# First layer of a fused block: condition rows and three more modulation tiles on TensorE, weight low halves on VectorE, modulation sums behind the value norm, gating loop reordered

## Chip, cores and metric

The kernel runs on one core of a Trainium2 chip. The metric is the device time of one execution in microseconds (us), the median of three runs. The engines are TensorE (PE in the views; its weight loads are PEld), VectorE (DVE), ScalarE (ACT), GpSimd (POOL) and SyncE (SP), whose queue issues the transfers.

## The reference, cut to what matters

The program is one block of two layers (AB, then CD) followed by a second block of two layers (feed-forward, token mixing, feed-forward). The change lies in the AB layer, for 512 tokens of x and 256 of a context that goes through the same weights with another condition row:

```
sh, sc, gt = split(silu(cond) @ w_mod + b_mod)         # cond is c for x, c_ctx for ctx
h = x * (1 + sc) + sh
a, ga, u, v, gb = split(h @ w_in)
ya = multiscale_pool(a) * silu(ga)                     # 4 groups, windows 2, 4, 8, 16
vn = (v - mean) * rsqrt(var + eps)                     # per head of 128
f  = w_s @ vn + b_s                                    # per head, chunks of 128 tokens
yb = u * f * silu(gb)
x  = layer_norm(ALPHA * x + gt * ([ya, yb] @ w_out))
```

The CD layer needs its own shift, scale and gate from the same condition rows. All is in fp32. A product of matrices is made of three fp32r matmuls: high half by high half, high by low, low by high.

## The kernel before

**Weights.** `wload` (L75) takes the next 128x1024 weight tile from a queue: a transfer into one of two buffers `ws`, the high half `wh` on ScalarE (L89) and the low half `wl = ws - wh` on the engine that `s.w_eng` names (L90). Five pairs wh, wl are kept. `s.w_eng` is GpSimd in the AB layer and stays so through the CD layer up to its output weights (L1072); elsewhere it is VectorE.

**Modulation.** 48 tiles of w_mod (24 for AB, 24 for CD) are 128 output channels each. A tile in `ON_PE` is loaded into `wm` and multiplied on TensorE by the silu of the condition (`pm`, L545). Any other is multiplied on VectorE, once for each condition row, with that row spread over all partitions (`junk`, L472, 128x1024, one such instruction for each row). The spread rows lie in `fbt`; they are loaded ready spread from `crow` (1 MB) and put through Silu on ScalarE (L561, L562).

**Stages of the AB layer.** (1) For the 8 channel chunks k: shift and scale tiles k and 8+k (`mods`), then h of the chunk as halves xH, xL and cH, cL (`modx`: L480 and L481 on ScalarE, L482 on VectorE), then 18 matmuls of the values `pv` (6 token tiles by 3). (2) The values are copied out (L596) and normalised by head (`bn_stats` L598, rsqrt L191 to L199, 24 scalings L607). (3) Gating, 4 heads g: projections of u and gb (`proj`, 24 matmuls of 512 columns into pa, 24 of 256 into pb), `pf` (the 128x128 matmul along the chunk), then sum, product, Silu and split into Y[4+g]. (4) Pooling, 4 groups g: projections a and ga, g+1 shifted sums of 800 columns on VectorE (L665), a first product `pp`, gate, split into Y[g]; the products of group g stand behind the projections of group g+1. (5) Output: 8 tiles m over all of Y, residual, layer norm in three segments, which runs into the CD layer.

**Order.** Modulation tiles 16 to 23 of AB (the gate) and all 24 of CD are a list of jobs; `wload` runs `s.rate` of them for each weight that it loads (2.2). They use parts of `xs` and `ctmp` as buffers. The program's order is only a start: a scheduler places the instructions on each engine, and every engine then works in that fixed order. Each engine waits at the first instruction that is not ready.

Of the kernel before, what the change touches and what calls it, by code (L numbers as in the profile page):

```python
# [9 lines left out]
F32 = mybir.dt.float32  # L10
# [3 lines left out]
ALU = mybir.AluOpType  # L14
# [7 lines left out]
ALPHA = 4.0 ** 0.25  # L22
ON_PE = (0, 8, 10, 13, 15)
HALF = (slice(0, 256), slice(256, 512))
# [7 lines left out]
class Net:  # L32
# [412 lines left out]
    def ab_weights(s):  # L445
        I = s.I
        for c in range(4):
            s.wpush(I["ab_v"][c], 1024)
        for i in (8, 12, 9, 13, 10, 14, 11, 15):
            s.wpush(I["ab_in"][i], 1024)  # L450
        s.wpush(I["pool_w"], 512)
        for i in (0, 4, 1, 5, 2, 6, 3, 7):
            s.wpush(I["ab_in"][i], 1024)
        for m in range(8):
            s.wpush(I["ab_out"][m], 1024)
# [55 lines left out]
    def ab(s):  # L511
        nc, tc, I = s.nc, s.tc, s.I
        s.psum(mm=range(6), t=(6, 7))
        s.w_eng = nc.gpsimd
        fbt = s.xp.tile([P, 4096], F32, tag="fb", name="fbt")
# [5 lines left out]
        C = [c_p.tile([P, 8, 256], F32R, tag="c" + t, name="c" + t) for t in "HL"]  # L521
        s.mods_start()
        b1 = c_p.tile([P, 16], F32, name="b1")
        nc.vector.tensor_copy(b1[:, 0:8], s.vec("ab_b", 0, 8))
        nc.vector.tensor_scalar(b1[:, 8:16], s.vec("ab_b", 8, 8), 1.0, None, op0=ALU.add)
        xs = s.xp.tile([P, 4096], F32, tag="x", name="xs")
        pv = [s.bank("pv") for _ in range(6)]

# [48 lines left out]
        spare = []  # L577

        def buf():
            spare.append(spare.pop(0))  # L580
            return spare[-1]
        spare += [xs[:, 3072:], ctmp[:, :1024], ctmp[:, 1024:]]
        nc.sync.dma_start(s.ident, I["ident"])
        nc.sync.dma_start(fbt[:, 2048:2560], I["sgu_b"])
# [3 lines left out]
        with tc.tile_pool(name="y", bufs=1, reuse_waits="tile") as yp, tc.tile_pool(name="yt", bufs=1, reuse_waits="tile") as tp:  # L588
# [32 lines left out]

            u = proj()
            for g in range(4):
                gb = proj()
                if g < 3:
                    u2 = proj()
                if g == 0:
                    s.jobs = [(lambda i=i: s.mod_dve(s.ab_m, I["ab_mod"], i, 2, fbt, buf)) for i in range(16, 24)]
                    s.jobs += [(lambda i=i: s.mod_dve(s.cd_m, I["cd_mod"], i, 2 if i < 16 else 1, fbt, buf)) for i in range(24)]
                G = tp.tile([P, 768], F32, tag="G", name="G")  # L630
                t_ = tp.tile([P, 768], F32, tag="T", name="T")
                pf = s.bank("pf", "t"), s.bank("pf", "t")
                for c in range(6):
                    nc.tensor.matmul(pf[c // 4][:, c % 4 * P:(c % 4 + 1) * P], vn[:, c, g], fbt[:, 2560 + g * P:2560 + (g + 1) * P], start=True, stop=True)
                for i, sl in enumerate(PARTS):
# [3 lines left out]
                    nc.vector.tensor_tensor(tt.rearrange("p (c i) -> p c i", i=P), pf[i][:, :n].rearrange("p (c i) -> p c i", i=P), bs, op=ALU.add)  # L639
                    nc.scalar.activation(G[:, sl], gb[i], AF.Silu)  # L640
                    nc.vector.tensor_tensor(tt, tt, u[i], op=ALU.mult)
                    nc.vector.tensor_tensor(tt, tt, G[:, sl], op=ALU.mult)
                    ysplit(4 + g, tt, sl)
                u = u2
# [59 lines left out]
            s.add_bias(s.cd_m, "cd_b", 0, 16)
            s.add_bias(s.cd_m, "cd_b", 16, 24, 1)
            nc.vector.tensor_scalar(s.cd_m[:, 8:16], s.cd_m[:, 8:16], 1.0, None, op0=ALU.add)

            s.gb = s.fc.tile([P, 2, 8, 2], F32, name="gb")
            for v in range(2):
                nc.vector.tensor_tensor(s.gb[:, 0, :, v], s.cd_m[:, 8:16, v], s.vec("ab_g", 0, 8), op=ALU.mult)  # L710
                nc.vector.tensor_tensor(s.gb[:, 1, :, v], s.cd_m[:, 8:16, v], s.vec("ab_lb", 0, 8), op=ALU.mult)
                nc.vector.tensor_tensor(s.gb[:, 1, :, v], s.gb[:, 1, :, v], s.cd_m[:, 0:8, v], op=ALU.add)
            ag = c_p.tile([P, 2, 8], F32, name="ag")
# [916 lines left out]
```

## Time and profile before

| | before |
|---|---|
| median of 3 runs | 2776.08 us (2770.22 to 2778.55) |
| profiled execution | 2773.9 us, its span 2772.1 us |
| TensorE busy | 2637.8 us (95%), 13676 instructions |
| VectorE busy | 1506.4 us (54%) |
| ScalarE busy | 1057.8 us (38%) |
| GpSimd busy | 322.3 us (12%) |
| chain that ended last | PE 76%, DVE 13%, ACT 3%, issue 3%, DMA 3% |

Times in the views are us from the span's start. "Busy" is time in which at least one instruction of the engine ran. What stands in brackets behind an instruction is the engine's idle time in front of it, and what ended it. The granted clock (PEclk) is given as a share of full speed: 1.00 is 2.4 GHz and 0.50 is 1.2 GHz.

### The profile page before, as it was taken

The page shows a single profiled execution, that of the slowest core. Times are in us where ns is not written, and L with a number is a line of the kernel's source. Part 1 is how long each engine was busy: PE and PEld are TensorE (multiplying, and loading weights), DVE is VectorE, ACT ScalarE, POOL GpSimd, SP SyncE. Part 2 cuts the span into 40 slices and gives each one's busy share as a digit, 9 for nine tenths or more (in the row PEclk, how much of TensorE's full clock was granted, in tenths as well). Part 3 has the DMA queues.
Part 4 walks back from the last instruction along what each step waited for, and adds up shares of the span by engine and source line. Part 5 has one row for each costly group of instructions (what it writes and reads, how often), then busy time and mean ns, then how long its engine had stood idle before and what let it go on. Part 6 is the DMA issues. An engine that isn't in the chain of part 4 may idle for free.

```text
span 2772.1 us, 36203 instructions
## 1 busy us (share of the span) xinstructions
PE 2637.8 (95%) x13676; PEld 2229.2 (80%) x13676; DVE 1506.4 (54%) x2886; ACT 1057.8 (38%) x1951; POOL 322.3 (12%) x300
## 2 busy tenths in 40 slices
PE   7898999998999998999999999999998998999998
PEld 6787987887888886877888888888886877888887
DVE  7885632888545353675853436634335467642334
ACT  4122543765443232444542224433223355432222
POOL 2324343002000020001200002000001000300000
PEclk9999999999999998999999999999999999999999
DMA  7353123005897246654693223962235665232321
GB/s 268 133 183 127 44 86 98 28 32 188 296 324 270 93 143 194 194 159 153 205 309 122 94 89 103 322 216 99 96 110 183 205 197 152 70 106 92 99 91 62
DMA packets 133966, 418.15 MB, mean 151 GB/s; under 512 B 17376, under 2 KB 20960, under 8 KB 133792
## 3 DMA queue, kind: packets, MB, share of 16 engines
q1 hardware_dynamic: 133792, 415.84, 45.3%
q8 instruction: 108, 1.77, 0.3%
q14 instruction: 66, 0.54, 0.1%
HBM read 314.32 MB, written 73.40 MB: 140 GB/s over the span
## 4 chain that ended last, share of the span: by engine, by line
PE 76%; DVE 13%; ACT 3%; issue 3%; DMA 3%; SPq 1%; POOL 0%; DVEq 0%; ACTq 0%; POOLq 0%
PE pd L146 6%; PE pd L145 6%; PE pd L144 6%; PE pg L144 5%; PE pg L145 5%; PE pg L146 5%; PE pu L145 5%; PE pu L146 5%; PE pu L144 5%; DVE junk L472 2%; PE pO L1256 1%; PE pq L144 1%; DVE x L310 1%; PE pq L145 1%; PE pq L146 1%
## 5 line engine op out<-in xcount | busy, mean ns | idle before, releaser
L89 ACT ACTIVATE wh<-ws 128x1024 fp32r<-128x1024 f32 (+2 forms) x335 | 345.6, 1034 | 865.5 <-PE pd L145 242.1
L90 DVE TENSOR_TENSOR wl<-ws,wh 128x1024 fp32r<-128x1024 f32 (+1 forms) x267 | 318.1, 1192 | 165.0 <-ACT wh L89 161.6
L144 PE MATMUL pg<-xH,wh 128*128 128x512 f32 x672 | 262.3, 390 | 0.0
L146 PE MATMUL pg<-xH,wl 128*128 128x512 f32 x672 | 261.7, 389 | 0.0
L145 PE MATMUL pg<-xL,wh 128*128 128x512 f32 x672 | 261.7, 389 | 0.0
L146 PE MATMUL pd<-hH,wl 128*128 128x512 f32 x632 | 249.7, 395 | 0.0
L144 PE MATMUL pd<-hH,wh 128*128 128x512 f32 x632 | 249.6, 395 | 0.0
L145 PE MATMUL pd<-hL,wh 128*128 128x512 f32 x632 | 249.6, 395 | 0.0
L145 PE MATMUL pu<-xL,wh 128*128 128x512 f32 x640 | 249.2, 389 | 0.0
L144 PE MATMUL pu<-xH,wh 128*128 128x512 f32 x640 | 249.1, 389 | 0.0
L146 PE MATMUL pu<-xH,wl 128*128 128x512 f32 x640 | 249.0, 389 | 0.0
L90 POOL TENSOR_TENSOR wl<-ws,wh 128x1024 fp32r<-128x1024 f32 (+1 forms) x68 | 171.1, 2522 | 328.7 <-ACT wh L89 320.9
L244 POOL TENSOR_TENSOR accf<-accf,sq 128x256 f32<-128x256 f32 x48 | 39.6, 846 | 1388.3 <-ACT sq L243 1388.3
L396 DVE TENSOR_TENSOR ht<-ht,pu 128x512 f32<-128x512 f32 x80 | 54.8, 685 | 183.4 <-PE pu L146 181.3
L146 PEld LDWEIGHTS pg<-xH,wl 128*128 128x128 f32 x672 | 126.1, 188 | 26.2
L144 PEld LDWEIGHTS pg<-xH,wh 128*128 128x128 f32 x672 | 126.2, 188 | 26.1
L145 PEld LDWEIGHTS pg<-xL,wh 128*128 128x128 f32 x672 | 126.2, 188 | 25.9
L146 PEld LDWEIGHTS pd<-hH,wl 128*128 128x128 f32 x632 | 118.6, 188 | 28.8
L145 PEld LDWEIGHTS pd<-hL,wh 128*128 128x128 f32 x632 | 118.6, 188 | 28.8
L144 PEld LDWEIGHTS pd<-hH,wh 128*128 128x128 f32 x632 | 118.6, 188 | 28.6
L144 PEld LDWEIGHTS pu<-xH,wh 128*128 128x128 f32 x640 | 120.1, 188 | 25.1
L146 PEld LDWEIGHTS pu<-xH,wl 128*128 128x128 f32 x640 | 120.1, 188 | 24.9
(616 smaller groups left out, 5978.5 us busy)
## 6 DMA issues: line engine op xcount, KB each, us to landing
ws<-ffn_gate SPq DMA_DIRECT2D x88, 512.0 KB, 3.5
ws<-ffn_up SPq DMA_DIRECT2D x88, 512.0 KB, 3.5
hl<-eh SPq DMA_DIRECT2D x64, 512.0 KB, 7.2
hl<-el SPq DMA_DIRECT2D x64, 512.0 KB, 6.8
ws<-ffn_down SPq DMA_DIRECT2D x64, 512.0 KB, 3.7
wh<-hl SPq DMA_DIRECT2D x64, 512.0 KB, 4.5
wl<-hl SPq DMA_DIRECT2D x64, 512.0 KB, 5.9
es<-wqk SPq DMA_DIRECT2D x32, 512.0 KB, 6.0
```

The source lines that it names most:

```text
L89: nc.scalar.activation(wh[:, :n], st[:, :n], AF.Copy)
L90: s.w_eng.tensor_tensor(wl[:, :n], st[:, :n], f(wh[:, :n]), op=ALU.subtract)
L144: mm(out, A[0], B[0], start=start, stop=False)
L145: mm(out, A[0], B[1], start=False, stop=False)
L146: mm(out, A[1], B[0], start=False, stop=stop)
L244: (eng or nc.gpsimd).tensor_tensor(acc[0], acc[0], sq, op=ALU.add)
L310: nc.vector.scalar_tensor_tensor(s.x[:, k, sl], fk, s.hg[post][:, k:k + 1], s.x[:, k, sl], op0=ALU.mult, op1=ALU.add)
L396: nc.vector.tensor_tensor(t, t, pu, op=ALU.mult)
L472: nc.vector.tensor_tensor_reduce(j, w, fbt[:, v * 1024:(v + 1) * 1024], 1.0, 0.0, op0=ALU.mult, op1=ALU.add, accum_out=dst[:, m, v:v + 1])
L1256: nc.tensor.matmul(o, vt(j), p[:, j, c0:], start=(x == 0 and j == 0), stop=(x == 1 and j == nj - 1))
```

## The change

- `ON_PE` holds 8 tiles in place of 5: of the 16 shift and scale tiles, 8 are now on VectorE (11 before). The value loop has tiles 1 and 9 on TensorE, and 13 no longer.
- The spread rows are no longer loaded. 16 matmuls `pr` (condition column spread, times the identity, 128 columns each) make them in four banks, and four ScalarE copies put them into `fbt`. The identity is loaded first, and `pv` takes its banks after `pr`.
- `s.w_eng` is VectorE in the AB layer, and so in the CD layer too, since nothing sets it before L1083 of the new kernel.
- Of the 24 value scalings, those of odd token tiles go to ScalarE (L608), and the order is by head.
- The jobs have three buffers of their own (`mj`), are placed behind the last VectorE scaling, and run 1.4 for each weight. CD's may run until the output stage.
- Gating: u of two heads is projected first; `pf`, its sum and the product with u stand ahead of the projection of gb. The weight order follows.

```diff
-ON_PE = (0, 8, 10, 13, 15)
+ON_PE = (0, 1, 8, 9, 10, 12, 14, 15)
...
-        s.w_eng = nc.gpsimd
+        s.w_eng = nc.vector
...
         for v in range(2):
-            row = fbt[:, v * 1024:(v + 1) * 1024]
-            nc.sync.dma_start(row, I["crow"][:, v * 1024:(v + 1) * 1024])
-            nc.scalar.activation(row, row, AF.Silu)
+            for h in range(2):
+                pr = s.bank("pr")
+                for j in range(4):
+                    nc.tensor.matmul(pr[:, j * P:(j + 1) * P], s.sc[:, 4 * h + j, v:v + 1].to_broadcast([P, P]), s.ident, start=True, stop=True)
+                nc.scalar.activation(fbt[:, v * 1024 + h * T:v * 1024 + (h + 1) * T], pr, AF.Copy)
         modx(0)
+        s.wload(1)
         mods(1)
+        pv = [s.bank("pv") for _ in range(6)]
...
+            nb = c_p.tile([P, 24], F32, name="nb")
+            nc.vector.scalar_tensor_tensor(nb, mv[:, :, 0], -1.0, rv, op0=ALU.mult, op1=ALU.mult)
+            for h in range(4):
+                for t in range(6):
                     j = t * 4 + h
-                    nc.vector.tensor_scalar(vn[:, t, h], vn[:, t, h], mv[:, j, 0:1], rv[:, j:j + 1], op0=ALU.subtract, op1=ALU.mult)
+                    if t % 2:
+                        nc.scalar.activation(vn[:, t, h], vn[:, t, h], AF.Identity, scale=rv[:, j:j + 1], bias=nb[:, j:j + 1])
+                    else:
+                        normed = nc.vector.tensor_scalar(vn[:, t, h], vn[:, t, h], mv[:, j, 0:1], rv[:, j:j + 1], op0=ALU.subtract, op1=ALU.mult)
...
+                    with tc.issue_after(normed.ins):
+                        s.mod_dve(*a, fbt, buf)
...
+            us = [proj(), proj()]
+            s.jobs = [after_v(s.ab_m, I["ab_mod"], i, 2) for i in range(16, 24)]
+            s.jobs += [after_v(s.cd_m, I["cd_mod"], i, 2 if i < 16 else 1) for i in range(24)]
+            s.rate = 1.4
...
-            while s.jobs:
+            while len(s.jobs) > 24:
                 s.jobs.pop(0)()
```

**Start of the program, TensorE.** Before, the two first modulation tiles are followed at once by the values (pm: modulation products, pv: values).

```order
L545 MATMUL pm<-sc,wm 128x2 x16
L144 MATMUL pv<-wh,xH 128x512 x2
L145 MATMUL pv<-wl,xH 128x512
L146 MATMUL pv<-wh,xL 128x512
L145 MATMUL pv<-wl,xH 128x512
```

After the change the sixteen `pr` and two more modulation tiles stand ahead of them.

```order
L563 MATMUL pr<-ident,sc 128x128
L545 MATMUL pm<-sc,wm 128x2 x8
L563 MATMUL pr<-ident,sc 128x128 x3
L545 MATMUL pm<-sc,wm 128x2 x8
L563 MATMUL pr<-ident,sc 128x128 x12
L545 MATMUL pm<-sc,wm 128x2 x8
L144 MATMUL pv<-wh,xH 128x512 x2
L545 MATMUL pm<-sc,wm 128x2 x8
L144 MATMUL pv<-wh,xH 128x512 x2
```

Moved: twelve of the sixteen spreads stand between the second modulation tile and the third, and the first value matmul behind them.

**The value norm, VectorE.** Before, modulation sums (junk) stand between the steps of the rsqrt (ysgu, tsgu); the scalings of the values are the last row.

```order
L193 TENSOR_TENSOR tsgu<-ysgu 128x24
L472 ISA junk,ab_m<-ctmp,fbt 128x1024
L472 ISA ab_m 128x1
L194 TENSOR_TENSOR tsgu<-tsgu,ve 128x24
L472 ISA junk,ab_m<-ctmp,fbt 128x1024
L472 ISA ab_m 128x1
...
L198 SCALAR_TENSOR_TENSOR tsgu<-tsgu,ve 128x24
L199 SCALAR_TENSOR_TENSOR ysgu<-tsgu,ysgu 128x24
L607 TENSOR_SCALAR xs<-xs,mv,ysgu 128x128 x24
```

After the change:

```order
L598 BN_AGGR mv<-bns 128x2 x24
L90 TENSOR_TENSOR wl<-ws,wh 128x1024
L600 TENSOR_SCALAR ve<-mv 128x24
L90 TENSOR_TENSOR wl<-ws,wh 128x1024
L191 TENSOR_SCALAR ysgu<-ve 128x24
L193 TENSOR_TENSOR tsgu<-ysgu 128x24
...
L199 SCALAR_TENSOR_TENSOR ysgu<-tsgu,ysgu 128x24
L603 SCALAR_TENSOR_TENSOR nb<-mv,ysgu 128x24
L610 TENSOR_SCALAR xs<-xs,mv,ysgu 128x128 x12
L472 ISA junk,ab_m<-mj,fbt 128x1024
```

Moved: eight modulation sums from inside the norm to behind it, and two low halves of weights into it; twelve of the scalings have left the engine.

**The last pooling group, VectorE.** Before (ctmp, fbt: the shifted sums; T: the gated product; yL: the low half of Y):

```order
L665 TENSOR_TENSOR ctmp<-ctmp 128x799
L665 TENSOR_TENSOR fbt<-ctmp 128x797
L665 TENSOR_TENSOR ctmp<-fbt 128x793
L665 TENSOR_TENSOR fbt<-ctmp 128x785
...
L688 SCALAR_TENSOR_TENSOR T<-pp,vecs,G 128x512
L688 SCALAR_TENSOR_TENSOR T<-pp,vecs,G 128x256
L234 TENSOR_TENSOR yL<-T,yH 128x512
```

After the change:

```order
L90 TENSOR_TENSOR wl<-ws,wh 128x1024
L674 TENSOR_TENSOR ctmp<-ctmp 128x799
L674 TENSOR_TENSOR fbt<-ctmp 128x797
L674 TENSOR_TENSOR ctmp<-fbt 128x793
L674 TENSOR_TENSOR fbt<-ctmp 128x785
...
L697 SCALAR_TENSOR_TENSOR T<-pp,vecs,G 128x512
L90 TENSOR_TENSOR wl<-ws,wh 128x1024
L234 TENSOR_TENSOR yL<-T,yH 128x512
```

Moved: a low half ahead of the sums and one between gate and split. All 56 modulation sums of the jobs stand ahead of these rows in both orders.

## Rows read from the trace of the kernel before

**Rows 1.** Windows: busy us of PE, PEld, DVE, ACT, POOL; PEclk; DMA share; GB/s.

```profile
100.00:120.00 20.00, 15.66 (x64) 12.94 (x65) 19.72 (x38) 2.28 (x5) 0.03 (x1) 0.75 0.37 131
160.00:180.00 20.00, 20.00 (x124) 17.98 (x123) 19.24 (x31) 6.42 (x11) 5.09 (x2) 1.00 0.53 192
...
72.00:250.00 178.00, 156.55 (x864) 135.87 (x864) 151.88 (x247) 40.06 (x67) 56.92 (x21) 0.92 0.47 163
```

**Rows 2.** Timeline, TensorE, stage of the values and first projections (start, us).

```profile
5.30 6.96 PE L545 MATMUL pm<-sc,wm 128*128 128x2 f32 x32 [5.30 <-DMA wm<-ab_mod]
...
24.30 1.93 PE L545 MATMUL pm<-sc,wm 128*128 128x2 f32 x16
...
67.51 0.39 PE L144 MATMUL pa<-xH,wh 128*128 128x512 f32 x1
...
72.97 0.28 PE L144 MATMUL pb<-cH,wh 128*128 128x256 f32 x1
...
75.79 0.39 PE L144 MATMUL pa<-xH,wh 128*128 128x512 f32 x1
```

**Rows 3.** Timeline, TensorE, from the value norm to the second head.

```profile
108.50 0.79 PE L144 MATMUL pa<-xH,wh 128*128 128x512 f32 x1 [4.34 <-DVE T L641]
...
125.13 1.50 PE L634 MATMUL pf<-fbt,xs 128*128 128x128 f32 x12
```

**Rows 4.** Timeline, TensorE, second half of pooling and first output tiles.

```profile
207.23 0.49 PE L144 MATMUL pp<-yH,wh 128*128 128x512 f32 x1 [2.15 <-ACT yH L233]
...
219.43 0.39 PE L144 MATMUL pa<-xH,wh 128*128 128x512 f32 x1
...
228.77 0.40 PE L144 MATMUL pa<-yH,wh 128*128 128x512 f32 x1
...
242.02 0.80 PE L144 MATMUL pp<-yH,wh 128*128 128x512 f32 x1 [8.87 <-ACT yH L233]
...
250.62 0.39 PE L144 MATMUL pa<-yH,wh 128*128 128x512 f32 x1
...
259.06 0.39 PE L144 MATMUL pa<-yH,wh 128*128 128x512 f32 x1
```

**Rows 5.** Timeline, ScalarE and VectorE, stage of the values.

```profile
23.73 0.82 ACT L480 ACTIVATE xH<-xs,ab_m 128x512 fp32r<-128x512 f32 x1 [6.78 <-DVE ab_m L549]
...
36.34 1.22 DVE L472 CUSTOM_DVE_ANT_0 junk<-wm,fbt 128x1024 bf16<-128x1024 f32 x1
...
61.82 0.81 ACT L480 ACTIVATE xH<-xs,ab_m 128x512 fp32r<-128x512 f32 x1 [2.54 <-DVE ab_m L549]
```

**Rows 6.** Timeline, GpSimd and VectorE, a low half and what ran beside it.

```profile
163.78 2.44 POOL L90 TENSOR_TENSOR wl<-ws,wh 128x1024 fp32r<-128x1024 f32 x1 [5.08 <-ACT wh L89]
...
164.01 3.30 DVE L472 CUSTOM_DVE_ANT_0 junk<-xs,fbt 128x1024 bf16<-128x1024 f32 x1
```

**Rows 7.** Timeline, VectorE, first and last of the stretched rows from 72 to 250 us.

```profile
72.03 2.53 DVE L472 CUSTOM_DVE_ANT_0 junk<-xs,fbt 128x1024 bf16<-128x1024 f32 x1
...
246.59 2.46 DVE L234 TENSOR_TENSOR yL<-T,yH 128x512 fp32r<-128x512 f32 x1 [0.68 <-ACT yH L233]
```

**Rows 8.** Timeline, VectorE, value norm.

```profile
65.78 4.74 DVE L598 BATCH_NORM_STATS2 bns<-xs 128x6 f32<-128x128 f32 x24 [0.89 <-ACT xs L596]
...
92.02 0.17 DVE L198 SCALAR_TENSOR_TENSOR tsgu<-tsgu,ve 128x24 f32<-128x24 f32 x1
...
92.44 8.27 DVE L607 TENSOR_SCALAR xs<-xs,mv,ysgu 128x128 f32<-128x128 f32 x24
```

**Rows 9.** Groups by line: low halves on GpSimd to 320 us, and, from the page, on VectorE.

```profile
L90 POOL TENSOR_TENSOR wl<-ws,wh 128x1024 fp32r<-128x1024 f32 (+1 forms) x33 | 88.8, 2697 | 180.0 <-ACT wh L89 175.5 <-PE pp L146 4.5
...
L90 DVE TENSOR_TENSOR wl<-ws,wh 128x1024 fp32r<-128x1024 f32 (+1 forms) x267 | 318.1, 1192 | 165.0 <-ACT wh L89 161.6
```

**Rows 10.** Timeline, layer norm: VectorE, and TensorE behind it.

```profile
321.44 2.30 DVE L198 SCALAR_TENSOR_TENSOR tab<-tab,vab 128x2 f32<-128x2 f32 x1
...
321.66 0.67 PE L488 MATMUL muab<-accaccf,ones 128*128 128x256 f32 x2 [2.08 <-DVE accaccf L509]
```

More of the change, by code (lines that the diff above doesn't have):

```diff
@@ L448, in ab_weights @@
             s.wpush(I["ab_v"][c], 1024)
-        for i in (8, 12, 9, 13, 10, 14, 11, 15):
+        for i in (8, 9, 12, 10, 13, 11, 14, 15):
             s.wpush(I["ab_in"][i], 1024)
@@ L522, in ab @@
         s.mods_start()
+        nc.sync.dma_start(s.ident, I["ident"])
         b1 = c_p.tile([P, 16], F32, name="b1")
@@ L526, in ab @@
         xs = s.xp.tile([P, 4096], F32, tag="x", name="xs")
-        pv = [s.bank("pv") for _ in range(6)]
         def tokx(k, t):
@@ L576, in ab @@
         ctmp = c_p.tile([P, 2048], F32, tag="cx", name="ctmp")
[L577 to L583, printed above, removed]
+        buf = lambda: c_p.tile([P, 1024], F32, tag="mj", name="mj", bufs=3)
         nc.sync.dma_start(fbt[:, 2048:2560], I["sgu_b"])
@@ L603, in ab @@
             rv = s.rsqrt(ve, 24, "sgu")
-            for t in range(6):
-                for h in range(4):
+            nb = c_p.tile([P, 24], F32, name="nb")
+            nc.vector.scalar_tensor_tensor(nb, mv[:, :, 0], -1.0, rv, op0=ALU.mult, op1=ALU.mult)
+            for h in range(4):
+                for t in range(6):
                     j = t * 4 + h
-                    nc.vector.tensor_scalar(vn[:, t, h], vn[:, t, h], mv[:, j, 0:1], rv[:, j:j + 1], op0=ALU.subtract, op1=ALU.mult)
+                    if t % 2:
+                        nc.scalar.activation(vn[:, t, h], vn[:, t, h], AF.Identity, scale=rv[:, j:j + 1], bias=nb[:, j:j + 1])
+                    else:
+                        normed = nc.vector.tensor_scalar(vn[:, t, h], vn[:, t, h], mv[:, j, 0:1], rv[:, j:j + 1], op0=ALU.subtract, op1=ALU.mult)
             def proj(ahead=4):
@@ L620, in ysplit, with after_v, run @@
                 s.split(Y[0][:, k, sl], Y[1][:, k, sl], src)
-            u = proj()
-            for g in range(4):
[L624 to L631, printed above, removed]
+            def after_v(*a):
+                def run():
+                    with tc.issue_after(normed.ins):
+                        s.mod_dve(*a, fbt, buf)
+                return run
+            us = [proj(), proj()]
+            s.jobs = [after_v(s.ab_m, I["ab_mod"], i, 2) for i in range(16, 24)]
+            s.jobs += [after_v(s.cd_m, I["cd_mod"], i, 2 if i < 16 else 1) for i in range(24)]
+            s.rate = 1.4
+            for g in range(4):
                 pf = s.bank("pf", "t"), s.bank("pf", "t")
@@ L634, in ab @@
                     nc.tensor.matmul(pf[c // 4][:, c % 4 * P:(c % 4 + 1) * P], vn[:, c, g], fbt[:, 2560 + g * P:2560 + (g + 1) * P], start=True, stop=True)
+                t_ = tp.tile([P, 768], F32, tag="T", name="T")
                 for i, sl in enumerate(PARTS):
@@ L639, in ab @@
                     nc.vector.tensor_tensor(tt.rearrange("p (c i) -> p c i", i=P), pf[i][:, :n].rearrange("p (c i) -> p c i", i=P), bs, op=ALU.add)
+                    nc.vector.tensor_tensor(tt, tt, us[g][i], op=ALU.mult)
+                gb = proj()
+                if g < 2:
+                    us.append(proj())
+                G = tp.tile([P, 768], F32, tag="G", name="G")
+                for i, sl in enumerate(PARTS):
                     nc.scalar.activation(G[:, sl], gb[i], AF.Silu)
[L641 to L644, printed above, removed]
+                    nc.vector.tensor_tensor(t_[:, sl], t_[:, sl], G[:, sl], op=ALU.mult)
+                    ysplit(4 + g, t_[:, sl], sl)
             LP = 800
             A, S1, S2 = ctmp[:, 0:LP], ctmp[:, LP:2 * LP], fbt[:, 3072:3072 + LP]
-            spare[:] = [xs[:, j * 1024:(j + 1) * 1024] for j in range(4)]
             nc.gpsimd.memset(ctmp, 0.0)
@@ L703, in ab @@
             nc.vector.tensor_scalar(s.ab_m[:, 16:24], s.ab_m[:, 16:24], 1.0 / ALPHA, None, op0=ALU.mult)
[L704 to L712, printed above, removed]
             ag = c_p.tile([P, 2, 8], F32, name="ag")
@@ L743, in ab @@
                 fin(m, 2, b)
+            while s.jobs:
+                s.jobs.pop(0)()
+            s.add_bias(s.cd_m, "cd_b", 0, 16)
+            s.add_bias(s.cd_m, "cd_b", 16, 24, 1)
+            nc.vector.tensor_scalar(s.cd_m[:, 8:16], s.cd_m[:, 8:16], 1.0, None, op0=ALU.add)
+            s.gb = s.fc.tile([P, 2, 8, 2], F32, name="gb")
+            for v in range(2):
+                nc.vector.tensor_tensor(s.gb[:, 0, :, v], s.cd_m[:, 8:16, v], s.vec("ab_g", 0, 8), op=ALU.mult)
+                nc.vector.tensor_tensor(s.gb[:, 1, :, v], s.cd_m[:, 8:16, v], s.vec("ab_lb", 0, 8), op=ALU.mult)
+                nc.vector.tensor_tensor(s.gb[:, 1, :, v], s.gb[:, 1, :, v], s.cd_m[:, 0:8, v], op=ALU.add)
             Ws = s.wlast(3)
@@ L1497, in prep_first @@
     vec("c", np.ascontiguousarray(cc.reshape(2, 8, P).transpose(2, 1, 0)).reshape(P, 16))
-    A["crow"] = np.ascontiguousarray(np.broadcast_to(cc.reshape(1, 2048), (P, 2048)))
     vec("ab_b", rows(i("ab_b_mod")))
```

## The prediction

> **What bounds the kernel now.** The page says TensorE 95% busy, and over most of the span it is at its pace. I read the windows first, 20 us at a time, to find where it isn't: nearly all loss lies in the first 340 us, the AB layer. The reader should compare the windows 100 to 120 and 160 to 180 [rows 1]: in one TensorE runs 64 matmul records at a granted clock of 0.75 while VectorE is busy 19.72 of 20 us, in the other 124 at 1.00. So VectorE holds TensorE up in some stretches, and TensorE is the bound in the others. The timeline then gives each loss against TensorE's own pace. That pace: one projection is 75.79 - 67.51 = 8.28 us, its 24 matmuls of 512 columns take 72.97 - 67.51 = 5.46 us, 0.2275 us each [rows 2]; an output tile is 259.06 - 250.62 = 8.44 us; a pooling product is 228.77 - 219.43 - 8.28 = 1.06 us [rows 4]; a head's `pf` is about 1.3 us (1.50 us for the twelve, the last overlapped) [rows 3].
>
> Three losses after the values end at 67.51:
> - Norm and first head: three projections end at 67.51 + 3 x 8.28 = 92.35, and `pf` of the second head starts at 125.13. Between them is work for 1.3 + 2 x 8.28 = 17.9 us; **14.9 us** are lost: TensorE waits for the scalings, then for T (4.34 us), and after each wait runs at half pace for a while [rows 2, 3].
> - Pooling product of group 1: a wait of 2.15 us, and from 207.23 to 219.43 12.20 us for 1.06 + 8.28; together **5.0 us** [rows 4].
> - Pooling product of the last group: from 228.77 to 250.62 21.85 us for 8.44 + 1.06; **12.4 us**, 8.87 of them one wait [rows 4].
>
> Why VectorE is late: it shares something with GpSimd. A modulation sum alone takes 1.22 us [rows 5]; one that starts 0.23 us after a low half of GpSimd took 3.30 us and ended 1.1 us after GpSimd's record did [rows 6]. From 72 to 250 us there are seventeen places with such stretched rows, the first 2.53 and the last 2.46 us [rows 7]; their excess over the same form alone is between 0.6 and 2.2 us and sums to 34.5 us of the 151.9 us that VectorE is busy there [rows 1].
>
> The Trainium skill (SBUF — State Buffer, "Who interferes with whom") says that a VectorE instruction with two SBUF inputs and a GpSimd instruction that reads SBUF exclude each other, and the later one blocks for the whole of the other. The 3.30 us row agrees. By that rule the stretch is gone once GpSimd's low halves are; by the row alone it might have another cause, and the sum would keep the 34.5 us (third rival).
>
> **The change part by part.**
>
> *Start and values (term A).* Before, ScalarE starts chunk 1 at 23.73 and chunk 7 at 61.82, and the first projection starts 5.7 us after that [rows 2, 5]. VectorE paces these six chunks. In them the change takes off one tile (two sums, 2.5 us) and three stretches by GpSimd's low halves (some 2.1 us each, 6.3), and adds two low halves (2 x 1.19 = 2.4 [rows 9]): 38.1 becomes 31.7 us. But chunk 1 needs tiles 1 and 9, which now stand behind the spreads on TensorE. At the start a `pm` record takes 6.96 / 32 = 0.2175 us, later 1.93 / 16 = 0.12 [rows 2]: the low and the high level, 1.2 and 2.4 GHz. A `pr` isn't in the trace; the nearest is `pf`, also 128 columns and two records a matmul: 1.3 / 6 = 0.22 us at the high level, twice that at the low one. Sixteen cost 3.5 to 7.0 us, and tiles 1 and 9 1.9 to 3.5 us each. Starting at 5.30, with the two old tiles (7.0), chunk 1 is ready between 5.3 + 7.0 + 3.5 + 3.8, with the two first value matmuls and a wait for their weight about 23, and 5.3 + 7.0 + 7.0 + 7.0 + 0.9 = 27.2. TensorE's own work is a second limit: behind the spreads (15.8 to 19.3) stand two tiles (3.8 to 7.0), 144 value matmuls (32.8) and four tiles (7.2), so the values can't end before 59.6 to 66.3. VectorE's limit is 23 to 27.2 + 31.7 + 5.7 = 60.4 to 64.6. I take 63.5, toward the slow ends, because a few waits come on top: **-4.0 us**, between -7 and +1.5. On SP's queue the identity now stands ahead of the first tile, an eighth of its bytes; that tile landed at 5.30, so it costs at most some 0.6 us of the range. The removed megabyte of `crow` and its two Silu are worth nothing by themselves: four copies of 512 columns replace them on a ScalarE that has room.
>
> The Trainium skill (TensorE: Matmul & The Clock Gate, "Part 1: The HAM clock gate") says that the array starts at the low level and rises after sustained work. The first records agree (0.2175 us each). By that rule the unbroken work from 5.30 could raise the clock within the spreads, and term A would be -7; the first 7 us of `pm` here did not raise it, so the sum goes by the slow ends.
>
> *Norm (term B).* bn_stats started 1.7 us ahead of the end of the values and took 4.74 us, the aggregates lasted to 72.03; then eight modulation sums and GpSimd's stretches spread the rsqrt, and the scalings ran from 92.44 to 100.7, 33.2 us after the values [rows 2, 7, 8]. Afterwards: 3.0 + 1.6 + two low halves 2.4 + eight small steps of about 0.2 us (spacing in front of 92.44) 1.6 + `nb` 0.2 + twelve scalings at 8.27 / 24 = 0.345, 4.1: VectorE is done 12.9 us after the values. ScalarE's twelve of 128 columns aren't in the trace: above nothing, and below the 0.82 us of 512 columns [rows 5]. The order is by head, so even at 0.82 the three of the first head are done 2.5 us after the rsqrt, and the others have a projection's time each; they cost nothing. Two u projections occupy TensorE for 16.6 us, so `pf` finds its values with 3 us to spare, and the first low half, ready 5.9 us after the values, is in time for the second u (8.3). T is formed under the gb projection. **-14.9 us**; 3 us of it are given back if VectorE is 6 us later.
>
> *Low halves and sums (terms C and D).* Does VectorE keep up to the end of pooling? All 56 job sums still stand ahead of the last pooling group in the order, so the later allowance for CD's brings nothing here. Ledger from the scalings on: 151.9 - 34.5 (stretch) - 9.8 (scalings 8.3, rsqrt 1.5) + 19 low halves x 1.19 (22.6) = 130.2 us [rows 1, 9]. From 63.5 + 12.9 = 76.4 that ends at 206.6; I add 4 us for copies of ScalarE between dependent steps (0.68 in front of 246.59 [rows 7]), so 210.6. TensorE alone: 63.5 + 16 x 8.28 + 4 x 1.3 + 4 x 1.06 + 8.44 = 213.9 for the first output tile, against 250.62. The two engines end within 3 us of each other, so C and D (5.0 + 12.4) come back except for what such a close race costs: I charge **3 us**, 0 to 12.
>
> *Layer norm (term E).* Two small VectorE steps of the rsqrt took 2.3 us beside GpSimd's low halves, and TensorE waited 2.08 us right behind [rows 10]. Low halves now stand at these two places, 1.19 us each: 2.1 us less. I take **-2 us**, 0 to -4.
>
> *CD layer.* Its low halves move too, some 35. TensorE is at its pace there and VectorE half idle until attention, so I cost them at nothing; their cover is five pairs of weights. If it fails, each is worth at most its 1.19 us.
>
> *Other edits.* The own buffers `mj` and the rate change when transfers start; a sum needs 1.22 us and its tile is asked for three tiles earlier. Queued behind a late one on VectorE would be a low half, then a projection. I cost it at nothing, inside the 3 us.
>
> **Sum.** -4.0 - 14.9 - 5.0 - 12.4 + 3 - 2 = -35.3 us on the profiled execution's 2773.9 us (span 2772.1): 2738.6. That execution lies 2.2 us under the median, so a median by the same sum is 2740.8; I say **2740**.
>
> **Rivals.**
> 1. *VectorE becomes the bound.* It loses GpSimd's help, and its order puts low halves behind steps that wait for ScalarE's Silu, hence for TensorE. For it: the two ends 3 us apart, VectorE busy 19 of 20 us in [rows 1]. Against: the low halves stand some 10 us ahead of their projections in the ledger. At 0.6 us of waiting for each of the 19, 11 us: 2751.
> 2. *The start gains nothing.* All spreads and tiles at the low level and one wait: values end at 69, term A +1.5: 2746.
> 3. *The waits only move: no change.* If the stretch has another cause and stays, the ledger is 164.7 us and ends at 245; TensorE then gets from the norm early and waits in pooling instead, and the first output tile ends near 249: 1.6 us gained there, 2 at the layer norm: 2772. For it: VectorE's load is what the change leaves in place. Against: each stretched row stands beside a low half of GpSimd.
> 4. *Slower.* A circle: projection waits for its low half, that stands behind T times G, which waits for Silu of the projection before. Every projection would pay; gains of 34 us and 8.3 us (0.3%) are lost from 2.7 us for each of the sixteen. The half pace after each wait would help it along. At 3.2 us each: 2787. Against: five pairs of weights cover four projections, 33 us.
>
> **How the numbers follow.** Forecast 0.62, rivals 0.17, 0.11, 0.05, 0.05. About 0.3% (8.3 us) is what can be told from no change; cases 1 and 2 lie 25 us and more below the median, so faster is 0.90, same 0.05, slower 0.05. All of A, B, C, D, E at their good ends (-7 - 14.9 - 17.4 - 4) gives 2733; with nothing more than rivals 1 and 2 halfway combined, 2755. Range 2732 to 2756.
>
> **What would show it.** Right: first projection at 61 to 66; no wait of TensorE over 1 us from there to the first output tile, PEclk 1.00; sums of 1.22 us throughout, no 3.3; the second output tile at 214 to 222; nothing of GpSimd's low halves before the mixing layers. Wrong: TensorE waiting for `wl` or T in the gating and pooling loops, VectorE without idle time from 64 to 215, or sums still stretched.

## The result and the profile after

The changed kernel takes 2745.32 us in the median of four runs (2738.18 to 2750.15); the kernel before, run beside it, took 2773.82. The ratio is 0.9894, interval [0.9866, 0.9922]: faster by 28 us or 1.1%, inside the predicted 2732 to 2756, 5 us above the forecast of 2740. The profiled execution took 2746.12 us, its span is 2744.2. On the page TensorE's busy time barely moves, and GpSimd loses nearly half of its own (322.3 us before):

```profile
PE 2644.8 (96%) x13756; PEld 2242.2 (82%) x13756; DVE 1506.5 (55%) x2923; ACT 1063.2 (39%) x1965; POOL 172.5 (6%) x240
```

The windows of the changed kernel that answer to [rows 1] (columns as there):

```profile
100.00:120.00 20.00, 19.10 (x118) 16.81 (x117) 19.79 (x36) 3.61 (x6) 0.00 (x0) 1.00 0.64 209
160.00:180.00 20.00, 20.00 (x114) 17.59 (x113) 18.94 (x33) 4.14 (x7) 0.00 (x0) 1.00 0.73 236
72.00:250.00 178.00, 177.10 (x1037) 156.21 (x1036) 148.15 (x274) 50.89 (x86) 6.53 (x9) 1.00 0.53 175
```

VectorE is as busy from 100 to 120 us as before (19.79 of 20), but TensorE now runs 118 matmul records there, not 64, at a granted clock of 1.00. Two engines can be full at once: a busy share doesn't say whose work is waited for. What changed inside VectorE's busy time is seen in its groups from 60 to 250 us (count, busy us, mean ns, idle before):

```profile
L472 DVE CUSTOM_DVE_ANT_0 junk<-mj,fbt 128x1024 bf16<-128x1024 f32 x56 | 68.4, 1221 | 1.6 <-DMA mj<-cd_mod 0.9
L90 DVE TENSOR_TENSOR wl<-ws,wh 128x1024 fp32r<-128x1024 f32 x25 | 31.1, 1249 | 4.8 <-ACT wh L89 4.7
...
L653 DVE TENSOR_TENSOR T<-T,G 128x256 f32<-128x256 f32 x4 | 1.7, 420 | 0.0
```

A modulation sum takes 1.22 us throughout, none 2.5 or 3.3 as in [rows 6, 7]. TensorE's waits from 60 to 350 us, the two longest (total us, times, longest):

```profile
PE pa L144 <- DVE T L646: 0.9, 1, 0.9
PE kv L144 <- ACT xH L480: 0.6, 1, 0.6
```

Of the wait of 4.34 us for T 0.9 is left; those of 2.15 and 8.87 us [rows 3, 4] are gone, and so is the one at the layer norm [rows 10].

It isn't faster everywhere. TensorE's timeline, which answers to [rows 2], and under it a window:

```profile
5.77 3.57 PE L545 MATMUL pm<-sc,wm 128*128 128x2 f32 x16 [1.67 <-DMA wm<-ab_mod]
9.20 1.63 PE L563 MATMUL pr<-ident,sc 128*128 128x128 f32 x6
10.62 3.41 PE L545 MATMUL pm<-sc,wm 128*128 128x2 f32 x16
13.89 5.12 PE L563 MATMUL pr<-ident,sc 128*128 128x128 f32 x24
18.85 1.84 PE L545 MATMUL pm<-sc,wm 128*128 128x2 f32 x16
...
26.19 0.63 PE L145 MATMUL pv<-wl,xH 128*128 128x512 f32 x1
26.61 0.63 PE L146 MATMUL pv<-wh,xL 128*128 128x512 f32 x1
...
67.82 0.39 PE L144 MATMUL pa<-xH,wh 128*128 128x512 f32 x1
```

```profile
20.00:30.00 10.00, 9.56 (x40) 8.30 (x40) 6.36 (x11) 5.02 (x8) 0.00 (x0) 0.66 0.54 189
```

The first projection starts at 67.82 us, 0.3 later than before, though VectorE no longer paces the chunks: TensorE is at work almost without a gap, first slowly (a `pm` record 0.21 us, at 18.85 us 0.115), then at a granted clock of 0.66 (value matmuls 0.42 us apart, where 0.23 is the full pace).

I cut each trace at two places: the first projection, and the first `spec` product of the CD layer (384.74 us before, 349.67 after). The three pieces changed by +0.3, -35.4 and +7.2 us. All runs of this study, cut alike (each ratio is against runs of the kernel before taken beside that run, medians 2773.8 to 2777.3, and not against the 2776.08 of the first row):

| run | median us | ratio to before | first projection | to `spec` | `spec` to end |
|---|---|---|---|---|---|
| before | 2776.08 | | 67.51 | 317.2 | 2387.4 |
| after | 2745.32 | 0.9894 [0.9866, 0.9922] | 67.82 | 281.9 | 2394.5 |
| e1 after, low halves on GpSimd | 2778.35 | 1.001 [1.0, 1.0019] | 74.60 | 311.4 | 2387.0 |
| e2 before, low halves on VectorE | 2743.93 | 0.9884 [0.9866, 0.9902] | 63.83 | 282.8 | 2391.5 |
| e3 after, rows of c loaded | 2743.0 | 0.988 [0.9863, 0.9896] | 64.33 | 282.7 | 2394.2 |
| e4 after, five tiles on TensorE | 2742.66 | 0.9883 [0.9864, 0.9901] | 68.45 | 279.6 | 2390.6 |
| e5 after, GpSimd reads for nothing | 2786.74 | 1.0037 [1.0024, 1.005] | 72.87 | 321.1 | 2396.8 |
| e6 after, GpSimd only writes | 2744.87 | 0.988 [0.9865, 0.9894] | 70.47 | 282.8 | 2388.7 |
| e7 after, low halves twice | 2746.65 | 0.989 [0.9875, 0.9904] | 70.85 | 281.4 | 2391.8 |
| e8 after, old start | 2742.15 | 0.9868 [0.9854, 0.9883] | 65.93 | 282.3 | 2391.0 |
| e9 after, again | 2743.45 | 0.988 [0.9863, 0.9896] | 68.76 | 283.3 | 2389.1 |
| e10 = e8, again | 2741.3 | 0.9869 [0.9852, 0.9885] | 63.30 | 281.9 | 2388.5 |
| e11 = e8, tails on VectorE | 2719.08 | 0.9789 [0.9772, 0.9806] | 66.15 | 283.1 | 2369.5 |
| e12 = e8, sums of squares on VectorE | 2725.8 | 0.982 [0.9804, 0.9837] | 62.80 | 284.7 | 2379.0 |

### The profile page after: what moved, and what is told of

Same layout as the page of the kernel before. It is cut to its first block, busy times and chain, and to the rows that moved or that the text cites. A ratio compares the mean times of both kernels' runs of the same rounds, so it can differ in the third digit from the quotient of the medians.

```text
span 2744.2 us, 36330 instructions
## 1 busy us (share of the span) xinstructions
PE 2644.8 (96%) x13756; PEld 2242.2 (82%) x13756; DVE 1506.5 (55%) x2923; ACT 1063.2 (39%) x1965; POOL 172.5 (6%) x240
## 5 line engine op out<-in xcount | busy, mean ns | idle before, releaser
L90 DVE TENSOR_TENSOR wl<-ws,wh 128x1024 fp32r<-128x1024 f32 (+2 forms) x327 | 390.1, 1194 | 228.7 <-ACT wh L89 224.1
L145 PEld LDWEIGHTS pu<-xL,wh 128*128 128x128 f32 x640 | 120.1, 188 | 24.9
L234 DVE TENSOR_TENSOR el<-es,eh 128x1024 fp32r<-128x1024 f32 x64 | 78.2, 1222 | 106.4 <-DMA hl<-el 80.1
```

Of the source, the lines that this page charges most:

```text
L90: s.w_eng.tensor_tensor(wl[:, :n], st[:, :n], f(wh[:, :n]), op=ALU.subtract)
L145: mm(out, A[0], B[1], start=False, stop=False)
L234: s.nc.vector.tensor_tensor(L, src, f(H), op=ALU.subtract)
```

## Experiments

**Which part does it: e1 and e2.** One line exchanged between the two kernels, `ab` of each:

```diff
-        s.w_eng = nc.vector
+        s.w_eng = nc.gpsimd
```

(e1, in the changed kernel; e2 is the reverse in the kernel before.)

> The changed kernel with one thing undone: the low halves of the AB and CD layers are on GpSimd again. Theory (GpSimd's low halves stretch VectorE's instructions beside them, 34.5 us of VectorE time from 72 to 250 us before the change): rows of VectorE beside a low half of GpSimd take up to 3.3 us again, VectorE's ledger grows from 130 to about 142 us (22.6 us of low halves less, some 34.5 of stretch more) and its end in the pooling moves from about 211 to 225 to 235 us; the first output tile ends near 235 instead of 217, the layer norm's rsqrt loses 2 to 4 us again: about 2762 us, 2754 to 2770. Rival (the stretch has another cause, or its waits lay in the order alone): VectorE only gets rid of 22.6 us and nothing is stretched, the time stays at 2745 within 4 us, or falls.

> The kernel before with one part of the change alone: the low halves of the AB and CD layers on VectorE, the rest in the old order. Theory (stretch by GpSimd): 34.5 us of stretch leave VectorE between 72 and 250 us and 22.6 us of low halves come, 12 us net; the norm's scalings come some 7 us earlier, the layer norm 2 to 4, the start 2 to 3: about 2758 us, 2750 to 2766, so roughly half of the gain is the engine and half the order. Rival (another cause of the stretch): VectorE gets 22.6 us more work where it is the bound, 2785 to 2796 us.

Measured: e1 is no faster than the kernel before, e2 as fast as the changed one. Both lie beyond what I expected of the theory: the engine isn't half of the gain but all of it, and the rest of the change is worth nothing, with it (e2 is as fast as the changed kernel) or without it (e1 is as slow as the kernel before; it gains 5.8 us from the first projection to `spec` and starts that projection 7.1 us later). In e1 TensorE waits again from 60 to 350 us, and the groups of VectorE show why:

```profile
PE pa L144 <- DVE T L646: 11.3, 3, 6.1
PE pf L639 <- DVE T L645: 4.2, 1, 4.2
PE muab L488 <- DVE accaccf L509: 2.0, 1, 2.0
PE bcab L214 <- DVE yab L199: 1.9, 1, 1.9
```

```profile
L472 DVE CUSTOM_DVE_ANT_0 junk<-mj,fbt 128x1024 bf16<-128x1024 f32 x56 | 83.2, 1485 | 2.3 <-DMA mj<-cd_mod 1.4
L653 DVE TENSOR_TENSOR T<-T,G 128x256 f32<-128x256 f32 x4 | 10.4, 2606 | 0.0
```

The 56 sums cost 14.8 us more than after (83.2 against 68.4), but nothing waits for a sum soon. The four products T times G of 256 columns took 2.61 us each, not 0.42, and for these TensorE waits. One of them and the low half beside it, from e1's timelines:

```profile
111.80 3.44 POOL L90 TENSOR_TENSOR wl<-ws,wh 128x1024 fp32r<-128x1024 f32 x1 [10.19 <-ACT wh L89]
112.92 2.60 DVE L653 TENSOR_TENSOR T<-T,G 128x256 f32<-128x256 f32 x1
```

The product starts 1.1 us into GpSimd's record and ends 0.3 us behind it, as if it had stood until GpSimd was through.

In e2 the norm is in the old order, with the sums between its steps, and is in time anyhow. A small step of the rsqrt, first in the kernel before, then in e2:

```profile
77.02 2.38 DVE L193 TENSOR_TENSOR tsgu<-ysgu 128x24 f32<-128x24 f32 x1
```

```profile
72.84 0.18 DVE L193 TENSOR_TENSOR tsgu<-ysgu 128x24 f32<-128x24 f32 x1
```

The scalings and the first projection of e2 (VectorE and TensorE):

```profile
82.44 6.25 DVE L607 TENSOR_SCALAR xs<-xs,mv,ysgu 128x128 f32<-128x128 f32 x24
```

```profile
63.83 0.39 PE L144 MATMUL pa<-xH,wh 128*128 128x512 f32 x1
```

The scalings end at 88.69; three projections from 63.83 end at 63.83 + 3 x 8.28 = 88.67. Steps without stretch brought the end forward, 33.2 us behind the values becoming 24.9: four small steps took 2.4 us each before and take 0.18 here.

**What GpSimd does to VectorE: e5, e6, e7.** Three edits of the changed kernel, each behind the low half in `wload` and in the AB layer alone (the condition for that is left out below, and the three are drawn together):

```diff
             s.w_eng.tensor_tensor(wl[:, :n], st[:, :n], f(wh[:, :n]), op=ALU.subtract)
+            nc.gpsimd.tensor_tensor(s.scr[:, :n], s.scr[:, :n], f(wh[:, :n]), op=ALU.subtract)   # e5
+            nc.gpsimd.tensor_tensor(s.scr[:, :1], s.scr[:, :1], f(wh[:, :1]), op=ALU.subtract)   # e6
+            for _ in range(3): nc.gpsimd.memset(s.scr, 0.0)                                      # e6
+            s.w_eng.tensor_tensor(wl[:, :n], st[:, :n], f(wh[:, :n]), op=ALU.subtract)           # e7
```

> The changed kernel with GpSimd work that nobody needs: behind each low half of the AB layer, which stays on VectorE, GpSimd subtracts the same 128x1024 piece of the weight from a scratch tile (two SBUF inputs, 1024 columns, as its low half of before), and nothing waits for the result. Theory (contention: VectorE's instructions with two SBUF inputs stand still while GpSimd reads): VectorE keeps the low halves and gets 1.1 to 1.4 us of stretch beside each of about 24 GpSimd records, 26 to 34 us, where it ends within a few us of TensorE: sums of 2.4 to 3.3 us again, first output tile 24 to 34 us later, 2768 to 2782 us. Rival (what cost time before was that the low halves came late from a slow engine, or the order): nobody waits for GpSimd here, 2745 within 4 us.

> As the run before, but GpSimd's piece is three memsets of the 128x1024 scratch tile (behind a one-column subtraction that ties them to the weight): as long on GpSimd (about 2.7 us), and it only writes SBUF. Theory (it is GpSimd's reading that stops VectorE): no stretched rows but for the one column, 2743 to 2749 us. Rival (any GpSimd instruction on SBUF stops VectorE's): as long as in the run before, 2765 or more.

> The changed kernel with each low half of the AB layer computed twice on VectorE, the second time over the first; GpSimd has nothing. This adds about 24 x 1.2 = 29 us to VectorE without any stretch. Theory (my ledger: VectorE ends within some 3 us of TensorE at the pooling): first output tile 20 to 30 us later than the 210 us of the changed kernel, waits of TensorE for VectorE in gating and pooling, 2765 to 2775 us. Rival (VectorE has more room than the ledger says, so that plain load is covered and only stretch hurts): 2745 to 2752.

In e5 nobody waits for GpSimd's subtraction, and 41 us are lost against the changed kernel, some 5 more than I expected at most; the low halves on VectorE beside GpSimd's record take 2.1 us, not 1.25. The groups of e5 (GpSimd 20 to 250 us, VectorE 60 to 250):

```profile
L92 POOL TENSOR_TENSOR scr<-scr,wh 128x1024 f32<-128x1024 f32 x24 | 70.3, 2931 | 169.1 <-ACT wh L89 168.8
...
L90 DVE TENSOR_TENSOR wl<-ws,wh 128x1024 fp32r<-128x1024 f32 x19 | 39.3, 2076 | 0.7 <-ACT wh L89 0.7
L657 DVE TENSOR_TENSOR T<-T,G 128x256 f32<-128x256 f32 x4 | 6.0, 1512 | 0.0
```

In e6 GpSimd is busy longer (88.2 us from 72 to 250, against 56.3 in e5) and costs nothing; groups of e6:

```profile
L94 POOL MEMSET scr<- 128x1024 f32 x87 | 83.1, 955 | 5.1
...
L476 DVE CUSTOM_DVE_ANT_0 junk<-mj,fbt 128x1024 bf16<-128x1024 f32 x56 | 68.4, 1222 | 2.0 <-DMA mj<-cd_mod 1.2
```

So it is GpSimd's subtraction, which reads SBUF, and neither its lateness nor its being busy; a memset, which only writes, costs nothing. (Each memset record is shorter, 0.955 us against 2.93, but the sums beside them aren't stretched by even that much.) The theory holds, the rivals of e5 and e6 fall.

e7 went to the rival. VectorE got 29 us of plain work more (groups and window of e7) and the time to `spec` didn't grow:

```profile
L90 DVE TENSOR_TENSOR wl<-ws,wh 128x1024 fp32r<-128x1024 f32 x24 | 29.4, 1226 | 2.6 <-ACT wh L89 2.6
L92 DVE TENSOR_TENSOR wl<-ws,wh 128x1024 fp32r<-128x1024 f32 x24 | 29.2, 1218 | 0.0
```

```profile
72.00:250.00 178.00, 176.17 (x1033) 155.75 (x1032) 173.37 (x325) 51.41 (x87) 8.85 (x9) 1.00 0.54 173
```

VectorE is busy 173.4 of 178 us here, more than in e5 (170.0), which loses 39 us on the same stretch. The scheduler knows of a longer list and puts the sums later: the last starts at 243.8 us, in the changed kernel at 188.5, and of the 56 sums 18 stand behind VectorE's first step on a pooling product instead of 5. It doesn't plan with a stretch: in e5 5 sums stand there, as in the changed kernel, and the steps behind them come late.

**The start: e3, e4, e8, e10.** e3 loads `crow` and puts it through Silu as before; e4 has the old table; e8 and e10 (the same kernel twice) have both:

```diff
-ON_PE = (0, 1, 8, 9, 10, 12, 14, 15)
+ON_PE = (0, 8, 10, 13, 15)
...
-            for h in range(2):
-                pr = s.bank("pr")
...
+            row = fbt[:, v * 1024:(v + 1) * 1024]
+            nc.sync.dma_start(row, I["crow"][:, v * 1024:(v + 1) * 1024])
+            nc.scalar.activation(row, row, AF.Silu)
```

> The changed kernel with the rows of c loaded from memory again and passed through Silu on ScalarE (1 MB more to load ahead of the first x), so TensorE has no spreads; the eight tiles stay on TensorE. The changed kernel's first projection started at 67.82 us, 0.3 after that of before, where I had taken 63.5. Theory (TensorE is the bound of the start: sixteen spreads at the low clock level take 6.4 us, and all behind is at TensorE's pace): first projection at 62 to 65 us, time 2740 to 2743. Rival 1 (VectorE paces the chunks, or loading does, so that TensorE's time at the start is covered): first projection at 67 to 69, 2744 to 2748. Rival 2 (a clock that falls anyhow: the granted clock of 0.63 to 0.69 between 20 and 30 us moves along): 66 to 68. The 7 us that the changed kernel gave back behind 385 us: if they are the scatter of single executions, this trace shows another number; if they come with the change, it shows 6 to 8 again.

> The changed kernel with the old five tiles on TensorE (0, 8, 10, 13, 15) instead of eight; the rows of c stay on TensorE. VectorE gets three tiles back, six sums, 7.3 us, and chunk 1 waits for four sums behind the spreads; TensorE gets rid of three tiles, 5.5 us and more at the low clock. Theory (in the changed kernel TensorE is the bound of the start by a little, VectorE by the ledger within 3 us of it): now VectorE is the bound, first projection at 69 to 72 us, 2747 to 2750. Rival (more tiles on TensorE bring nothing, since the spreads set the start): first projection at 64 to 68, 2741 to 2745.

> The changed kernel with the old start: rows of c loaded, five tiles on TensorE; all else as changed. Two runs had the rows loaded and started the first projection at 63.8 (old order and five tiles) and 64.3 us (changed order and eight tiles), two had them made on TensorE: 67.8 (eight tiles) and 68.5 (five). Theory (the spreads on TensorE cost 3.5 to 4.5 us, the three more tiles bring nothing): first projection at 63.5 to 65, 2739 to 2743 us. Rival (tiles and rows work together): 66 or later, 2743 to 2747.

> The changed kernel with the old start again (rows of c loaded, five tiles on TensorE), on the same chip as the changed kernel: theory, 3 to 4 us faster than it (its first projection starts at about 64 instead of 67.8), 2739 to 2743; rival, no difference that can be told.

With the rows loaded, the first projection starts between 62.80 and 66.15 us, 64.4 in the mean of six traces (e2, e3, e8, e10, e11, e12); with spreads between 67.82 and 68.76, 68.3 in the mean of three (the changed kernel twice, and e4; e5 to e7 have other work in the start, and e1 its low halves on GpSimd). So the spreads cost 4 us there, and the three more tiles nothing that shows (64.33 with eight, 62.80 to 66.15 with five). e3's theory holds, in start and time. e4's expectation missed on both sides: neither did VectorE's six sums make the start later nor did fewer tiles make it earlier. The start of e10:

```profile
5.58 6.96 PE L544 MATMUL pm<-sc,wm 128*128 128x2 f32 x32 [5.58 <-DMA wm<-ab_mod]
22.82 1.84 PE L544 MATMUL pm<-sc,wm 128*128 128x2 f32 x16
...
63.30 0.39 PE L144 MATMUL pa<-xH,wh 128*128 128x512 f32 x1
```

e8 and e10 are one kernel and start 2.6 us apart. In both TensorE waits for xH of a chunk for 2.2 us; behind that wait e8 goes on at half pace and e10 doesn't (first e8, then e10):

```profile
35.47 0.80 PE L144 MATMUL pv<-wh,xH 128*128 128x512 f32 x1 [2.17 <-ACT xH L480]
```

```profile
35.20 0.50 PE L144 MATMUL pv<-wh,xH 128*128 128x512 f32 x1 [2.15 <-ACT xH L480]
```

The granted clock from 30 to 40 us is 0.83 in e8 and 1.00 in e10, from 40 to 60 us 0.91 and 1.00. e11 and e12, whose starts are alike, show the same two cases: 0.83 and 0.91 with a start at 66.15, 1.00 throughout with one at 62.80.

In the times the 4 us of the spreads can't be told: e10 is 2.2 us under e9 in the median, and their intervals overlap.

**The changed kernel again: e9.**

> The changed kernel itself once more, beside the two that follow in time: 2742 to 2748 us. Its trace says what scatters from one execution to the next: in the nine traces so far the stretch from the queries of the first mixing layer's second group to the third takes 82.7 to 84.7 us and the same one of the second mixing layer 82.3 to 85.2, in kernels whose mixing layers are the same. If that scatter made the 7 us which the changed kernel's trace lost behind 385 us, this trace loses another amount (0 to 7).

The stretch from `spec` to the end took 2389.1 us, in the first trace 2394.5; e8 and e10, one kernel, took 2391.0 and 2388.5. The 7 us that the first trace gave back are largely scatter: e9 gives back 1.8.

**The same cure elsewhere: e11 and e12.** On top of e8, in `sq_add` (both) and in `mix` (e11 alone):

```diff
-            (eng or nc.gpsimd).tensor_tensor(acc[0], acc[0], sq, op=ALU.add)
+            (eng or nc.vector).tensor_tensor(acc[0], acc[0], sq, op=ALU.add)
...
-        s.w_eng = nc.gpsimd
+        s.w_eng = nc.vector
```

> The kernel of the run before, and the same cure where GpSimd's reading still stands beside VectorE: the sums of squares in the tails of all layers and the last four low halves of each mixing layer go to VectorE as well. In the changed kernel's trace TensorE waits there for a chain of small VectorE steps: 6.2 us in four waits, 5.5 in two, 3.6 and 1.8 in one each, 17 us. Theory (these steps are stretched by GpSimd's sums too): a third to a half of these waits goes, 5 to 9 us: 2733 to 2738. Rival (the added sums of 0.4 us each stand in VectorE's way in the tails as long as the stretch did): 2739 to 2745.

> The run before had two edits on the old-start kernel and took 22 us less than it, more than twice what I expected. This one has the sums of squares alone on VectorE; the four low halves of each mixing layer are back on GpSimd. Theory (the sums stand in the tails, where a chain of VectorE steps feeds TensorE: rows of the two steps of the tail before the second layer fell from 0.82 and 0.69 to 0.48 us): nearly all of it, 2719 to 2724 us. Rival (the low halves of the mixing layers, where TensorE waits for a chain of sigmoid scans and copies): less than half, 2730 to 2739.

e11 is the fastest kernel of the study, 22 us under e10 and 2.1% under the kernel before: more than twice what I expected. e12 keeps 14 to 15 of the 22 us, between theory and rival, and the four low halves of each mixing layer are worth the other 7 to 8. It is the same stretch: in e12 each of these eight low halves has a VectorE row beside it that takes 1.86 to 2.48 us, where 0.42 to 0.48 us are usual, and e11 has none. One of the eight, from e12's timelines:

```profile
2334.77 2.35 POOL L90 TENSOR_TENSOR wl<-ws,wh 128x1024 fp32r<-128x1024 f32 x1 [2.25 <-ACT wh L89]
2334.91 2.48 DVE L310 SCALAR_TENSOR_TENSOR x<-fb,vecs,x 128x256 f32<-128x256 f32 x1
```

VectorE's groups over the whole span, first of e10, then of e11:

```profile
L264 DVE SCALAR_TENSOR_TENSOR xL<-x,vecs,xH 128x256 fp32r<-128x256 f32 x96 | 64.4, 672 | 0.8 <-ACT xH L263 0.6
L310 DVE SCALAR_TENSOR_TENSOR x<-fb,hg_ffn,x 128x256 f32<-128x256 f32 x64 | 35.1, 570 | 0.0
L310 DVE SCALAR_TENSOR_TENSOR x<-fb,vecs,x 128x256 f32<-128x256 f32 x32 | 21.4, 689 | 0.0
```

```profile
L264 DVE SCALAR_TENSOR_TENSOR xL<-x,vecs,xH 128x256 fp32r<-128x256 f32 x96 | 45.6, 478 | 1.3 <-ACT xH L263 0.8
L244 DVE TENSOR_TENSOR acc<-acc,sq 128x256 f32<-128x256 f32 x84 | 35.0, 417 | 0.0
L310 DVE SCALAR_TENSOR_TENSOR x<-fb,hg_ffn,x 128x256 f32<-128x256 f32 x64 | 29.0, 478 | 0.0
L244 DVE TENSOR_TENSOR accf<-accf,sq 128x256 f32<-128x256 f32 x48 | 18.2, 420 | 2.0 <-ACT sq L243 2.0
L310 DVE SCALAR_TENSOR_TENSOR x<-fb,vecs,x 128x256 f32<-128x256 f32 x32 | 14.4, 477 | 0.0
```

VectorE takes on 53 us of sums and gets 32 us of stretch back on these three groups; it ends with more work (1526.0 us against 1513.4) and the kernel is faster: the tails are a chain that TensorE waits behind, and a step there now takes 0.48 us each time. TensorE's waits from `spec` to the end, added up, are 78.3 us in e10 and 65.4 in e11, 13 of the 19 us by which that stretch is shorter; the other 6 aren't traced to rows.

## Why the prediction was right, and where it wasn't

**Stretch and its cure: right, and the whole of the gain.** From the first projection to `spec` I had -14.9 - 5.0 - 12.4 + 3 - 2 = -31.3 us; measured were -35.4, and -33.9 in the second trace. Of the signs I had named, no wait over 1 us, sums of 1.22 us and the second output tile (218.77 us, 214 to 222 expected) came; the first projection (67.82, not 61 to 66) didn't. That GpSimd's low halves stretch VectorE's rows (third rival, 0.05, against it) is shown by e1 and e2, and by e5 against e6. The rule of the Trainium skill (SBUF — State Buffer, "Who interferes with whom"), that a VectorE instruction with two SBUF inputs contends with a GpSimd instruction that reads SBUF and not with one that only writes, agrees with e5 (2.08 us for a low half of 1.25) and e6 (1.22 us for a sum).

**Norm (term B): right in size, wrong in what brings it.** I worked it out from the sums behind the norm, the scalings on ScalarE and two u projections ahead. After, the second head's values are in time. But they are in e2 too, in the old order: what brings them is that the stretch is gone. And in e1 the new order has no wait left for the values and almost none in pooling, and 11.3 and 4.2 us of waits for T in gating instead: the third rival's picture, waits that only move, is nearly right for the order alone.

**Terms C and D: right.** Both waits are gone. **The close race (+3): no race.** In e7 29 us more on VectorE cost nothing, so VectorE had ten times the room that my ledger gave it. The ledger took the 56 sums as fixed; the scheduler moves them. The first rival falls with it.

**Layer norm (term E): undersized.** Each of the two stretched steps had a wait of TensorE behind it, in the kernel before of 2.1 us (`muab`, in [rows 10]) and 1.9 us (`bcab`); e1 has both again, and neither is left after. -4, not -2: the step that failed counted one of two waits.

**Start (term A): wrong by 4 to 5 us.** Predicted -4.0, measured +0.3 and +1.3. VectorE's side agrees: with low halves moved and rows loaded, the start is 3.1 us earlier (64.4 against 67.51). The step that failed is TensorE's limit, which I had as 59.6 to 66.3 and expected toward 63.5. The spreads are inside it, at its slow end: the first tile came 0.5 us later, and thirty `pr` records took 1.63 + 5.12 us. What it left out is that value matmuls run at half pace too: it has all 144 at 0.2275 us, but the nine from 24.76 to 28.75 us were 0.44 us apart, 1.9 us more (granted clock 0.66 from 20 to 30 us). The trace of the kernel before showed it already, with value matmuls 0.43 us apart up to 24.3 us. Waits of 1.2 us for xH come on top. The Trainium skill (TensorE: Matmul & The Clock Gate, "Part 1: The HAM clock gate") would have the array faster after sustained work; here 13 us of nearly unbroken small matmuls went by before a record of two columns took 0.115 us and not 0.21, so the better end that I drew from it was off by 7 us. That the array ran at the lower of its two levels there is read from the records alone; the granted clock shows 1.00. The second rival (the start gains nothing, 2746) is what happened there.

**CD layer and other edits at nothing: right.** From `spec` to the end the kernels without e11's and e12's edits lie between 2387.0 and 2396.8 us, and one kernel differs from itself by 5.4. The two with CD's low halves on GpSimd (before and e1) are the shortest, 2387.4 and 2387.0, but not by the CD layer: from `spec` to its layer norm (the first `mucd`) they take 237.9 and 238.2 us, the others 238.2 to 239.0. So moving them cost under 1 us; the other differences lie behind, where these kernels don't differ.

So the number is right in part by luck. The sum was -35.3 us, the profiled executions differ by -27.9: the start was overrated by 4.3 us and the rest of the layer underrated by 4.1, which cancel, and the 7.2 us behind `spec` are for the most part scatter (1.8 in the second trace). Two figures of the rivals don't follow from their terms: 3.2 us for each of sixteen projections on top of 2740 is 2791, not 2787, and rivals 1 and 2 in full, not halfway, make about 2757, near the 2755. No conclusion rests on them. What stays open is what makes up the 1.8 us behind `spec` in e9, and why the granted clock falls behind the same wait in one execution of a kernel and not in another (e8, e10).

## What to carry to other kernels

Look for rows of one form with two durations, and for what runs on GpSimd in the long ones: an elementwise step given to GpSimd to relieve VectorE can cost VectorE more than the step itself (here 1 to 2 us of stretch for 1.2 us of work), and the cost falls on whatever VectorE happens to be doing, the urgent steps too. Before a change of many parts is believed part by part, undo or apply the cheapest part by itself: here one line carried everything (e2), and the parts that moved order were worth nothing (e1). A busy engine isn't yet the bound: add plain work to it and see if the time moves.

## What the runs showed of the hardware

GpSimd's memsets of 128x1024 (0.955 us each, 87 of them) beside VectorE left its sums at 1.22 us; GpSimd's subtraction with two SBUF inputs, 24 times, cost 39 us of path. A stretched VectorE row ends with GpSimd's record or shortly behind it, however short its own work is: 0.42 us became 2.60 in e1, 0.18 became 2.38 in the kernel before. In the windows from 0 to 20 us the granted clock shows 1.00 while TensorE's two-column records take 0.21 us, against 0.115 later; that column doesn't tell such a start apart, the rows do. A row needn't have two tensors as inputs to be stretched: of the 24 value scalings of the kernel before (one tensor and two per-partition columns) one took 2.37 us beside GpSimd's low half, the median 0.33; in e2, where GpSimd has none, the longest took 0.34.
